# The opening of a decoder block in written order: norm weights spread by TensorE, small products ordered by readiness

## The chip, the core and the metric

The kernel runs on one core of one Trainium2 chip. The time is the device time of one execution in microseconds (us). A profile is one execution recorded by the hardware profiler: what each engine did and when. TensorE (PE) multiplies matrices and also transposes, by a product with the identity; VectorE (DVE), ScalarE (ACT) and GpSimd (POOL) do elementwise work; SyncE (SP) issues transfers (DMA). PSUM is the memory that TensorE writes.

## The reference, cut to what matters

A block with two attention branches on 528 rows (16 meta tokens ahead of 512 tokens), width 1024. The change concerns only how `u` comes about, and the columns of the common projection that are needed first: `cq` (256), `ckv` (128), `k_pe_raw` (32) and `f_logit` (16), 432 columns together, called the small projection here. `fq` and `fk` follow it.

```
u = rmsnorm(h, pre_norm_g[l])
proj = u @ w_in[l]
(cq, ckv, k_pe_raw, z_mla, fq, fk, fv, f_logit, z_fox, gate_a, gate_b) = jnp.split(proj, split_idx, axis=-1)

q = (rmsnorm(cq, mla_q_norm_g[l]) @ w_uq[l])...
kv = (rmsnorm(ckv, mla_kv_norm_g[l]) @ w_ukv[l])...
k_pe = rope(k_pe_raw, pos)[:, None]
...
log_f = jax.nn.log_sigmoid((f_logit + fox_forget_b[l]).astype(jnp.float32)).transpose(0, 2, 1)
cum = jnp.cumsum(log_f, axis=-1)
```

## The kernel before

Products of float32 are made as three: both factors are split into a high part (a cast to fp32r by ACT) and a low part (the difference, by `split_lo`, L118), and high·high, high·low and low·high are added up in one accumulator. Names ending in `h` and `l` are these parts. A product's two inputs stand behind the arrow, its accumulator ahead of it: `psm<-wsh,uTl` is a product of the small projection.

The opening goes over five tiles of rows: T0 to T3 with 128 tokens each, T4 with the 16 meta rows. Each tile passes these steps:

- `ht` is loaded; ACT sums its squares into `st`, DVE multiplies by the root and by the norm's weights `gb` and gets `hn`.
- TensorE transposes `hn` in two halves of four blocks into `pt` (PSUM, two buffers); ACT casts the high part `uTh`, DVE subtracts for the low part `uTl`.
- 24 products (8 pieces of the width, three each) give `psm` (PSUM, two buffers): 432 columns, for T4 only 176. Its weights `wsh` and `wsl` are made from `wsr`, which comes in four chunks.
- ACT sums the squares of psm's parts, DVE normalizes them and makes the rotary terms `tm`, all into `sm`.
- TensorE transposes `sm` into `pc` (PSUM, one buffer: a 48-row piece and up to three of 128). ACT and DVE take from it `cTh`, `cTl`, `kpT` and `fT`.

In front of and between these lie the products of the first pair of heads: `fq` (24 products, 512 wide) and `fk` (two halves of 24 products, 272 and 256 wide), whose weights come as `wraw` and are split into `wh` (ACT) and `wl` (POOL). Behind them come `v`, `pg`, `ppe` and the rest, whose accumulators are taken in turn from one pool of three (`accp`), fq and fk included. `fa` and `ch` are the forget gates' logarithms and their running sum (a scan on DVE), `KPH` and `KPL` the parts of `kpT`, `hlk` the parts of `fk`.

`gb` needs the same 1024 weights on all 128 partitions; two DMAs on SP's queue, behind T0's rows, write them there (0.5 MB). The low parts `wsl` go by turns to POOL and DVE. The code of the opening calls whole steps (`front`, `back`) tile by tile, in the order T0, T1, T4, T2, T3, and the scheduler sets the order in which each engine gets the instructions.

Of the kernel before, what the change touches and what calls it, by code (L numbers as in the profile page):

```python
# [54 lines left out]
def block_kernel(ctx: ExitStack, tc: tile.TileContext, x, meta_tokens, pre_norm_g, w_in, fox_forget_b,  # L55
# [38 lines left out]
    def tps(*a):  # L94
        nc.tensor.transpose(*a)
# [21 lines left out]
    def split_lo(eng, lo, src, hi):  # L117
        eng.tensor_tensor(out=lo, in0=src, in1=f32(hi), op=ALU.subtract)  # L118
# [171 lines left out]


    lctx = ExitStack()
    with ExitStack() as ph:
# [27 lines left out]
        wsh = pa1.tile([128, KD, NSM], F32R, tag="wsh", name="wsh")  # L321
        wsl = pa1.tile([128, KD, NSM], F32R, tag="wsl", name="wsl")
        nsm0 = NSM - NH
        for c in range(4):
# [6 lines left out]
            nc.scalar.copy(hi, r)
# [15 lines left out]
        def rstd(dst, ss, n, epsc, rows):
            nc.scalar.activation(dst, ss, AF.Sqrt, bias=eps_t[:rows, epsc : epsc + 1], scale=1.0 / n)
# [2 lines left out]
        def front(t):
            rows, d0 = (128, META + 128 * t) if t < 4 else (META, 0)
            ht = hts[t]
            hn = pa.tile([128, D], F32, tag="hn", name=f"hn{t}")
            st1 = pa.tile([128, 16], F32, tag="st1", name=f"st1_{t}")
            parts = [slice(0, D)]
            if t == 0:

                parts = halves
                for i, sl in enumerate(parts):  # L360
                    nc.scalar.activation(hn[:, sl], ht[:, sl], AF.Square, accum_out=st1[:, 2 + i : 3 + i])
                nc.vector.tensor_scalar(out=st1[:, 0:1], in0=st1[:, 2:3], scalar1=1.0 / D, scalar2=EPS, op0=ALU.mult,
                                        op1=ALU.add)
                nc.scalar.activation(st1[:, 1:2], st1[:, 3:4], AF.Sqrt, bias=st1[:, 0:1], scale=1.0 / D)
                nc.vector.reciprocal(st1[:, 1:2], st1[:, 1:2])
            else:
                nc.scalar.activation(hn[:rows], ht[:rows], AF.Square, accum_out=st1[:rows, 0:1])
                rstd(st1[:rows, 1:2], st1[:rows, 0:1], D, 0, rows)
            for sl in parts:
                nc.vector.scalar_tensor_tensor(out=hn[:rows, sl], in0=ht[:rows, sl], scalar=st1[:rows, 1:2],  # L370
                                               in1=gb[:rows, sl], op0=ALU.mult, op1=ALU.mult)
            for half in range(2):
                pt = ppt.tile([128, 4, 128], F32, tag="pt", name=f"pt{t}_{half}")
                for kk in range(4):
                    k = 4 * half + kk
                    tps(pt[:, kk, :rows], hn[:rows, 128 * k : 128 * k + 128], ident[:rows, :rows])
                dh = uTh[:, 4 * half : 4 * half + 4, d0 : d0 + rows]
                dl = uTl[:, 4 * half : 4 * half + 4, d0 : d0 + rows]
                nc.scalar.copy(dh, pt[:, :, :rows])
                split_lo(nc.vector, dl, pt[:, :, :rows], dh)  # L380

        def back(t):

            rows, d0, q0 = (128, META + 128 * t, 0) if t < 4 else (META, 0, R_Q)
            psm = pps.tile([128, NSM], F32, tag="psm", name=f"psm{t}")
            passes(psm[:, q0:], lambda k: uTh[:, k, d0 : d0 + 128], lambda k: uTl[:, k, d0 : d0 + 128],
                   lambda k: wsh[:, k, :], lambda k: wsl[:, k, :], KD, slice(q0, NSM))
            sm = pa.tile([128, NSM], F32, tag="sm", name=f"sm{t}")
            st2 = pa.tile([128, 16], F32, tag="st2", name=f"st2_{t}")
            for a, b, i in ((0, R_Q, 0), (R_Q, R_Q + R_KV, 1)):  # L390
                if a < q0:
                    continue
                nc.scalar.activation(sm[:rows, a:b], psm[:rows, a:b], AF.Square, accum_out=st2[:rows, i : i + 1])
                rstd(st2[:rows, 2 + i : 3 + i], st2[:rows, i : i + 1], b - a, 0, rows)
                nc.vector.scalar_tensor_tensor(out=sm[:rows, a:b], in0=psm[:rows, a:b], scalar=st2[:rows, 2 + i : 3 + i],
                                               in1=gq[:rows, a:b], op0=ALU.mult, op1=ALU.mult)
            k0 = R_Q + R_KV
            tm = pa.tile([128, 2, 2, 16], F32, tag="tm", name=f"tm{t}")
            for i in range(2):
                for cs in range(2):  # L400
                    nc.vector.tensor_tensor(out=tm[:rows, i, cs], in0=psm[:rows, k0 + 16 * i : k0 + 16 * i + 16],
                                            in1=rt[:rows, t, 2 * i + cs], op=ALU.mult)
            nc.vector.tensor_tensor(out=sm[:rows, k0 : k0 + 32].rearrange("p (a b) -> p a b", a=2), in0=tm[:rows, 0],
                                    in1=tm[:rows, 1], op=ALU.add)
            nc.scalar.copy(sm[:rows, k0 + 32 :], psm[:rows, k0 + 32 :])
            pc = pps.tile([128, 4, 128], F32, tag="pc", name=f"pc{t}", bufs=1)
            i0 = q0 // 128
            for i in range(i0, 3):
                tps(pc[:, i, :rows], sm[:rows, 128 * i : 128 * i + 128], ident[:rows, :rows])
            tps(pc[0 : ROPE + NH, 3, :rows], sm[:rows, k0:NSM], ident[:rows, :rows])  # L410
            ds = slice(d0, d0 + rows)
            nc.scalar.copy(cTh[:, i0:3, ds], pc[:, i0:3, :rows])
            split_lo(nc.vector, cTl[:, i0:3, ds], pc[:, i0:3, :rows], cTh[:, i0:3, ds])
            nc.scalar.copy(kpT[:, ds], pc[0:ROPE, 3, :rows])
            nc.scalar.activation(fT[:, ds], pc[ROPE : ROPE + NH, 3, :rows], AF.Identity, bias=fb)
# [14 lines left out]
        nc.vector.scalar_tensor_tensor(out=fa[:, 1], in0=fT, scalar=0.0, in1=fa[:, 0], op0=ALU.min, op1=ALU.subtract)  # L430
        nc.vector.tensor_tensor_scan(out=fa[:, 0], data0=fa[:, 1], data1=fa[:, 2], initial=0.0, op0=ALU.add,
# [811 lines left out]
```

## Time and profile before

| | us |
|---|---|
| median of 3 runs | 623.63 (622.18 to 624.98) |
| the profiled execution's own time | 623.18 |
| its span | 621.3 |
| PE busy in the span | 600.1 (97%) |
| ACT busy | 384.0 (62%) |
| DVE busy | 381.8 (61%) |
| POOL busy | 188.9 (30%) |

The span goes from the first to the last recorded instruction; 1.9 us of the execution lie around it. Rows of the timeline read: start, duration, engine, line, operation, out<-in, partitions x elements, count, and in brackets the idle time of the engine before it with what ended it. Rows of groups give busy time and mean nanoseconds of one, then the idle time ahead. Rows of the chain give start, length and group.

### The profile page before, as it was taken

Reading aid. Unit: us, or ns where it says so; the run is one execution under the profiler, and the core shown is the slowest. Engines: PE = TensorE matmul, PEld = TensorE weight load, DVE = VectorE, ACT = ScalarE, POOL = GpSimd, SP = SyncE. Lnnn points to the kernel's source line nnn. Section 1 sums busy time; section 2 is a strip of 40 time slices with the busy share of each in tenths; the row PEclk is TensorE's granted clock in tenths of the full one; section 3 lists DMA queues with packets and bytes.
Section 4 is the critical chain, followed back from the end, with each engine's and each line's share of the span. In section 5 each row is a group of like instructions: output and inputs, shape, how many; then the busy total and the mean of one; then the engine's idle time right before and its main releaser. Section 6 shows DMA issues by size and latency. Waiting matters only on the chain.

```text
span 621.3 us, 11569 instructions
## 1 busy us (share of the span) xinstructions
PE 600.1 (97%) x4058; PEld 492.9 (79%) x4058; DVE 381.8 (61%) x1015; ACT 384.0 (62%) x838; POOL 188.9 (30%) x237
## 2 busy tenths in 40 slices
PE   3999999999999999999999999999999999999996
PEld 2879787978988889889889888887888865565885
DVE  3746668367466566674774774676977865556133
ACT  5656677379477576774884784776767654444421
POOL 3234544634444353352444353420000000003700
PEclk9999999999999999999999999999999999999998
DMA  8442576876666577467357586567252137332202
GB/s 284 129 85 52 128 139 175 188 192 163 161 136 140 142 148 157 125 167 180 97 142 172 137 145 161 137 162 216 66 157 80 35 89 250 101 111 93 102 34 103
DMA packets 204842, 85.15 MB, mean 137 GB/s; under 512 B 122788, under 2 KB 197924, under 8 KB 204784
## 3 DMA queue, kind: packets, MB, share of 16 engines
q1 hardware_dynamic: 204784, 84.41, 53.7%
q8 instruction: 32, 0.52, 0.4%
q14 instruction: 26, 0.21, 0.1%
HBM read 54.95 MB, written 4.00 MB: 95 GB/s over the span
## 4 chain that ended last, share of the span: by engine, by line
PE 88%; ACT 3%; DMA 3%; DVE 3%; POOL 2%; issue 1%; SPq 0%; DVEq 0%; ACTq 0%; POOLq 0%
PE pg L92 14%; PE z L92 13%; PE v L92 8%; PE st L92 7%; PE po L92 7%; PE fq L92 7%; PE fk L92 7%; PE py L92 6%; PE ov L92 5%; PE yx L92 3%; PE psm L92 3%; DMA wraw<-in_w_in_dram 2%; PE yy L92 2%; PE mq L92 2%; ACT wh L142 1%; PE mk L92 1%
## 5 line engine op out<-in xcount | busy, mean ns | idle before, releaser
L118 POOL TENSOR_TENSOR wl<-wraw,wh 128x1024 fp32r<-128x1024 f32 (+1 forms) x60 | 133.0, 2219 | 299.2 <-ACT wh L142 288.3
L142 ACT CAST wh<-wraw 128x1024 fp32r<-128x1024 f32 (+1 forms) x74 | 72.9, 986 | 84.8 <-issue 35.3
L708 ACT ACTIVATE sf<-sf,nb 128x144 f32<-128x144 f32 (+3 forms) x128 | 71.9, 565 | 3.4 <-DVE nb L698 3.4
L736 ACT ACTIVATE pn<-sf,ri 128x128 f16<-128x128 f32 (+3 forms) x128 | 61.9, 551 | 15.2 <-ACT sf L708 13.8
L737 DVE SCALAR_TENSOR_TENSOR pn<-sf,ri,pn 128x128 f16<-128x128 f32 (+3 forms) x128 | 65.6, 554 | 7.4 <-ACT pn L736 7.4
L92 PE MATMUL pg<-uTh,wh 128*128 128x512 f32 x128 | 51.9, 406 | 0.0
L92 PE MATMUL z<-uTh,wh 128*128 128x512 f32 x128 | 50.9, 398 | 0.0
L92 PE MATMUL z<-uTh,wl 128*128 128x512 f32 x128 | 50.1, 392 | 0.0
L92 PE MATMUL z<-uTl,wh 128*128 128x512 f32 x128 | 50.1, 391 | 0.0
L92 PE MATMUL pg<-uTh,wl 128*128 128x512 f32 x128 | 50.0, 391 | 0.0
L92 PE MATMUL pg<-uTl,wh 128*128 128x512 f32 x128 | 49.9, 390 | 0.0
L92 PE MATMUL st<-hlk,hlq 64*128 64x272 f32 (+3 forms) x480 | 48.6, 307 | 1.1 <-DVE nb L698 0.9
L698 DVE CUSTOM_DVE_ANT_0 sf<-st,maskt 128x272 f32<-128x272 f32 (+2 forms) x128 | 48.4, 434 | 0.0
L92 PE MATMUL py<-g,yw 128*128 128x512 f16 x192 | 42.6, 379 | 0.6 <-DVE yw L1006 0.6
L92 PEld LDWEIGHTS st<-hlk,hlq 64*128 64x128 f32 x480 | 35.7, 185 | 8.1 <-DVE nb L698 2.6
L92 PE MATMUL fk<-uTl,wh 128*128 128x256 f32 (+1 forms) x128 | 36.6, 286 | 0.0
L92 PE MATMUL v<-uTh,wh 128*128 128x256 f32 (+1 forms) x128 | 36.5, 285 | 0.0
L92 PE MATMUL fk<-uTh,wh 128*128 128x256 f32 (+1 forms) x128 | 36.5, 285 | 0.0
L92 PE MATMUL fk<-uTh,wl 128*128 128x256 f32 (+1 forms) x128 | 36.5, 285 | 0.0
L92 PE MATMUL v<-uTl,wh 128*128 128x256 f32 (+1 forms) x128 | 36.4, 285 | 0.0
L92 PE MATMUL v<-uTh,wl 128*128 128x256 f32 (+1 forms) x128 | 36.4, 285 | 0.0
L92 PEld LDWEIGHTS <-yw 128*128 128x128 f16 x192 | 17.8, 97 | 22.7 <-DVE yw L1006 1.1
(291 smaller groups left out, 1503.3 us busy)
## 6 DMA issues: line engine op xcount, KB each, us to landing
wraw<-in_w_in_dram SPq DMA_DIRECT2D x56, 512.0 KB
yraw<-in_w_br_fox_dram SPq DMA_DIRECT2D x8, 512.0 KB
yraw<-in_w_br_mla_dram SPq DMA_DIRECT2D x8, 512.0 KB
wraw<-in_w_out_dram SPq DMA_DIRECT2D x8, 512.0 KB
pt<-pn SPq DMA_TRANSPOSE x128
xr<-in_x_dram SPq DMA_DIRECT2D x4, 512.0 KB
out_dram<-yo SPq DMA_DIRECT2D x8, 256.0 KB
QP<-qpe_dram SPq DMA_DIRECT2D x7, 256.0 KB
```

What stands on the lines that cost most here:

```text
L92: nc.tensor.matmul(*a, **k)
L118: eng.tensor_tensor(out=lo, in0=src, in1=f32(hi), op=ALU.subtract)
L142: nc.scalar.copy(wh[:, :n], raw[:, :n])
L698: nc.vector.tensor_tensor_reduce(out=sf_of(h, b)[:, c0 : c0 + w], in0=ps[h][:, o : o + w], in1=maskt[:, m0 : m0 + w], scale=-scale, scalar ...
L708: nc.scalar.activation(sf, sf, AF.Exp, bias=sums["nb"][:, h, b : b + 1], scale=-1.0, accum_out=sums["su"][:, h, b : b + 1])
L736: nc.scalar.activation(hi, sf, AF.Copy, scale=rib)
L737: nc.vector.scalar_tensor_tensor(out=lo, in0=sf, scalar=rib, in1=hi, op0=ALU.mult, op1=ALU.subtract)
```

## The change

The opening stands under a manual schedule: on PE, ACT, DVE, POOL and SP the instructions now run in the order in which the code is written. The steps of a tile are cut into `square`, `norm`, `turn` (transposes), `psm`, `sums`, `norms` and `back`, and the code calls them one by one. Further:

- The norm's weights are loaded as one row, `grow` (4 KB), by ACT's DMA queue. TensorE multiplies a column of ones with it: `gb[0]`, `gb[1]`, two products 512 wide in PSUM, in two of the three accumulators. Ahead of them stand four products of ones (`dark`) whose result is not used; they take the third.
- `hn` is made in halves for every tile, since `gb` is in two PSUM tiles.
- The 24 products of the small projection go by chunk of the weights: high·high, low·high, high·low; for T0 the last two chunks' products with `wsl` come at the end.
- `wsl` of chunk 0 is made by POOL, of chunks 1 to 3 by DVE; the low parts of the first fq and fk weights (`qu.make`, `ku.make`) by DVE instead of POOL.
- Of one psm, ACT makes both sums and roots first (`sums`), then DVE both normalizations (`norms`); before they took turns.
- The tiles go in the order T0, T1, T2, T3, T4, and fq begins behind T4's psm.

```diff
+        ph.enter_context(tc.manual_schedule(engines={E_.PE, E_.Activation, E_.DVE, E_.Pool, E_.SP}))
...
+        grow = pa1.tile([1, D], F32, tag="grow", name="grow")
+        nc.scalar.dma_start(grow, pre_norm_g[0:1])
...
-        gb = pa1.tile([128, D], F32, tag="gb", name="gb")
-        for sl in halves:
-            nc.sync.dma_start(gb[:, sl], pre_norm_g[0:1, sl].broadcast_to([128, 512]))
...
-        qk = q_fox(0) + k_fox(0)
-        for f, t in ((front, 0), (front, 1), (back, 0), (front, 4), (front, 2), (back, 1), (front, 3), (back, 2)):
-            f(t)
-        run(qk[:3])
-        back(3)
-        run(qk[3:7])
-        back(4)
...
+        ORD = [(k, c) for c in range(4) for k in ("hh", "lh", "hl")]
...
+        dark = acc("dark")
+        for _ in range(4):
+            mm(dark, ALL1, ALL1.unsqueeze(1).broadcast_to([128, 4, 128]), start=True, stop=True)
+        gb = [acc(f"gb{i}") for i in range(2)]
+        for i, sl in enumerate(halves):
+            mm(gb[i], one, grow[:, sl], start=True, stop=True)
+
+        T[0].square()
+        w_hi(0)
+        w_lo(0, nc.gpsimd)
+        T[0].norm()
+        low = [T[0].turn(i) for i in range(2)]
...
+        T[3].psm(ORD[8:])
+        qu.make(nc.vector)
+        T[4].psm(ORD)
+        T[2].back()
+        T[3].sums()
+        ku.make(nc.vector)
+        T[3].norms()
+        run(q0[:4])
+        T[4].sums()
+        T[4].norms()
+        T[3].back()
+        run(q0[4:])
+        T[4].back()
         nc.scalar.activation(fa[:, 0], fT, AF.Abs)
         nc.scalar.activation(fa[:, 0], fa[:, 0], AF.Exp, scale=-1.0)
+        run(k0[:8])
...
-        run(qk[7:])
+        run(k0[8:])
```

Four places show what this moves. On ACT, around the last two tiles' `back`, before the change (`pc_419` and `psm_444` are T2's pc and T3's psm, `pc_486` T3's pc):

```order
L412 CAST cTh<-pc_419 128x3x128
L414 COPY kpT<-pc_419 32x128
L415 ACTIVATE fT<-pc_419,fb 16x128
L393 ACTIVATE sm_469,st_3_470<-psm_444 128x256
L348 ACTIVATE st_3_470<-st_3_470,eps_t 128x1
L393 ACTIVATE sm_469,st_3_470<-psm_444 128x128
L348 ACTIVATE st_3_470<-st_3_470,eps_t 128x1
L405 COPY sm_469<-psm_444 128x16
L412 CAST cTh<-pc_486 128x3x128
```

And after it (`pc_493` is T2's pc, `psm_396` T3's psm, `wh_464` and `wh_509` the high parts of fq's and fk's weights):

```order
L142 CAST wh_464<-wraw_257 128x1024
L453 CAST cTh<-pc_493 128x3x128
L455 COPY kpT<-pc_493 32x128
L456 ACTIVATE fT<-pc_493,fb 16x128
L425 ACTIVATE sm_502,st_3_503<-psm_396 128x256
L426 ACTIVATE st_3_503<-st_3_503,eps_t 128x1
L425 ACTIVATE sm_502,st_3_503<-psm_396 128x128
L426 ACTIVATE st_3_503<-st_3_503,eps_t 128x1
L428 COPY sm_502<-psm_396 128x16
L142 CAST wh_509<-wraw_322 128x1024
```

The order of the steps is the same here; what is new is fk's `wh` right behind T3's sums, and that T2's pc, for which the first `cTh` waits, now stands behind T4's products on TensorE.

On DVE, the same place before:

```order
L118 TENSOR_TENSOR cTl<-pc_419,cTh 128x3x128
L349 RECIPROCAL st_3_470<-st_3_470 128x1
L395 SCALAR_TENSOR_TENSOR sm_469<-psm_444,st_3_470,gq 128x256
L349 RECIPROCAL st_3_470<-st_3_470 128x1
L395 SCALAR_TENSOR_TENSOR sm_469<-psm_444,st_3_470,gq 128x128
L401 TENSOR_TENSOR tm_479<-psm_444,rt 128x16 x4
L403 TENSOR_TENSOR sm_469<-tm_479 128x32
L118 TENSOR_TENSOR cTl<-pc_486,cTh 128x3x128
```

And after:

```order
L118 TENSOR_TENSOR wl_465<-wraw_257,wh_464 128x1024
L118 TENSOR_TENSOR cTl<-pc_493,cTh 128x3x128
L118 TENSOR_TENSOR wl_510<-wraw_322,wh_509 128x1024
L436 TENSOR_TENSOR tm_513<-psm_396,rt 128x16 x4
L438 TENSOR_TENSOR sm_502<-tm_513 128x32
L442 RECIPROCAL st_3_503<-st_3_503 128x1
L443 SCALAR_TENSOR_TENSOR sm_502<-psm_396,st_3_503,gq 128x256
L442 RECIPROCAL st_3_503<-st_3_503 128x1
L443 SCALAR_TENSOR_TENSOR sm_502<-psm_396,st_3_503,gq 128x128
```

Fk's low part `wl_510` now stands between T2's `cTl` and T3's normalization.

On TensorE, the pieces of T3's pc (`pc_486`) lay one by one between products of fq and of T4's psm (`psm_507`) before:

```order
L92 MATMUL fq_434<-uTh,wh_430 128x512
L95 MATMUL pc_486<-ident,sm_469 128x128 x2
L92 MATMUL fq_434<-uTl,wh_430 128x512
...
L92 MATMUL fq_434<-uTh,wl_431 128x512
L95 MATMUL pc_486<-ident,sm_469 128x128
L92 MATMUL psm_507<-wsh,uTh 128x176
L92 MATMUL psm_507<-wsl,uTh 128x176
L95 MATMUL pc_486<-ident,sm_469 48x128
```

After, T4's psm (`psm_468`) comes first, then T2's pc, twelve products of fq, and T3's pc (`pc_549`) in one piece:

```order
L92 MATMUL psm_468<-wsl,uTh 128x176 x2
L95 MATMUL pc_493<-ident,sm_425 48x128
L95 MATMUL pc_493<-ident,sm_425 128x128 x3
L92 MATMUL fq_523<-uTh,wh_464 128x512
...
L92 MATMUL fq_523<-uTh,wl_465 128x512
L95 MATMUL pc_549<-ident,sm_502 48x128
L95 MATMUL pc_549<-ident,sm_502 128x128 x3
L92 MATMUL fq_523<-uTh,wh_464 128x512
```

Twelve products now stand between T2's pc and T3's, and twelve behind; before, 21 of fq's 24 stood ahead of the end of T4's psm.

On DVE behind the opening, `hlk` of fk's second half (`fk_606` before, `fk_622` after) has changed places with the scan and `ch`. Before:

```order
L430 SCALAR_TENSOR_TENSOR fa<-fT,fa 16x528
L118 TENSOR_TENSOR hlk_603<-fk_606,hlk_603 128x256
L431 SCALAR_TENSOR_TENSOR fa<-fa 16x528
L435 SCALAR_TENSOR_TENSOR ch<-fa,ch 16x528
L606 TENSOR_REDUCE vsc_730<-v_705 128x1
```

After:

```order
L541 SCALAR_TENSOR_TENSOR fa<-fT,fa 16x528
L542 SCALAR_TENSOR_TENSOR fa<-fa 16x528
L546 SCALAR_TENSOR_TENSOR ch<-fa,ch 16x528
L118 TENSOR_TENSOR hlk_607<-fk_622,hlk_607 128x256
L716 TENSOR_REDUCE vsc_747<-v_722 128x1
```

The subtraction that frees fk's second accumulator now stands behind the scan (the second `fa` row) and `ch`.

More of the change, by code (lines that the diff above doesn't have):

```diff
@@ L292, in block_kernel @@
     lctx = ExitStack()
+    E_ = mybir.EngineType
     with ExitStack() as ph:
+        ph.enter_context(tc.manual_schedule(engines={E_.PE, E_.Activation, E_.DVE, E_.Pool, E_.SP}))
         pa = ph.enter_context(tc.tile_pool(name="pa", bufs=2))
@@ L345, in block_kernel, with w_hi, w_lo @@
         kpT = pal.tile([ROPE, L], F32, tag="kpT", name="kpT")
+        wsh = pa1.tile([128, KD, NSM], F32R, tag="wsh", name="wsh")
+        wsl = pa1.tile([128, KD, NSM], F32R, tag="wsl", name="wsl")
+        def w_hi(c):
+            nc.scalar.copy(wsh[:, 2 * c : 2 * c + 2, :], wsr[c])
+        def w_lo(c, eng=nc.vector):
+            sl = slice(2 * c, 2 * c + 2)
+            split_lo(eng, wsl[:, sl, :], wsr[c], wsh[:, sl, :])
         def rstd(dst, ss, n, epsc, rows):
@@ L349, in rstd @@
             nc.vector.reciprocal(dst, dst)
[L351 to L373, printed above, removed]
@@ L374, in front @@
                 for kk in range(4):
                     k = 4 * half + kk
[L376 to L415, printed above, removed]
@@ new lines, in turn, with psm @@
+                return self.low
+            def psm(self, plan):
+                q0 = self.q0
+                if not hasattr(self, "ps"):
+                    self.ps = pps.tile([128, NSM], F32, tag="psm", name=f"psm{self.t}")
+                    self.n = 0
+                us = slice(self.d0, self.d0 + 128)
+                for kind, c in plan:
+                    for k in (2 * c, 2 * c + 1):
+                        u, w = ((uTh, uTl)[kind[0] == "l"], (wsh, wsl)[kind[1] == "l"])
+                        mm(self.ps[:, q0:], u[:, k, us], w[:, k, q0:], start=(self.n == 0), stop=(self.n == 3 * KD - 1))
+                        self.n += 1
@@ new lines, in sums @@
+            def sums(self):
+                t, r, q0, psm = self.t, self.rows, self.q0, self.ps
+                self.sm = sm = pa.tile([128, NSM], F32, tag="sm", name=f"sm{t}")
+                self.st2 = st2 = pa.tile([128, 16], F32, tag="st2", name=f"st2_{t}")
+                for a, b, i in ((0, R_Q, 0), (R_Q, R_Q + R_KV, 1)):
+                    if a >= q0:
+                        nc.scalar.activation(sm[:r, a:b], psm[:r, a:b], AF.Square, accum_out=st2[:r, i : i + 1])
+                        nc.scalar.activation(st2[:r, 2 + i : 3 + i], st2[:r, i : i + 1], AF.Sqrt, bias=eps_t[:r, 0:1],
+                                             scale=1.0 / (b - a))
+                nc.scalar.copy(sm[:r, R_Q + R_KV + ROPE :], psm[:r, R_Q + R_KV + ROPE :])
@@ new lines, in back @@
+            def back(self):
+                t, r, q0, sm, ds = self.t, self.rows, self.q0, self.sm, self.ds
+                pc = pps.tile([128, 4, 128], F32, tag="pc", name=f"pc{t}", bufs=1)
+                i0, k0 = q0 // 128, R_Q + R_KV
+                tps(pc[0 : ROPE + NH, 3, :r], sm[:r, k0:NSM], ident[:r, :r])
+                for i in range(i0, 3):
+                    tps(pc[:, i, :r], sm[:r, 128 * i : 128 * i + 128], ident[:r, :r])
+                nc.scalar.copy(cTh[:, i0:3, ds], pc[:, i0:3, :r])
+                split_lo(nc.vector, cTl[:, i0:3, ds], pc[:, i0:3, :r], cTh[:, i0:3, ds])
+                nc.scalar.copy(kpT[:, ds], pc[0:ROPE, 3, :r])
+                nc.scalar.activation(fT[:, ds], pc[ROPE : ROPE + NH, 3, :r], AF.Identity, bias=fb)
@@ new lines, in block_kernel @@
+        w_hi(0)
+        w_lo(0, nc.gpsimd)
+        T[0].norm()
+        low = [T[0].turn(i) for i in range(2)]
+        low[0]()
+        low[1]()
+        w_hi(1)
+        w_lo(1)
+        T[1].square()
+        w_hi(2)
+        w_hi(3)
+        T[0].psm(ORD[:6])
+        T[1].norm()
+        T[0].psm([("hh", 2), ("lh", 2)])
+        low = [T[1].turn(i) for i in range(2)]
+        w_lo(2)
+        w_lo(3)
+        T[0].psm([("hh", 3), ("lh", 3), ("hl", 2), ("hl", 3)])
+        low[0]()
+        low[1]()
@@ new lines, in block_kernel @@
+        T[2].square()
+        qu.load()
+        T[1].psm(ORD[:4])
+        T[0].sums()
+        T[2].norm()
+        T[1].psm(ORD[4:8])
+        low = [T[2].turn(i) for i in range(2)]
+        low[0]()
+        T[0].norms()
+        low[1]()
+        T[1].psm(ORD[8:])
+        T[3].square()
+        ku.load()
+        T[2].psm(ORD[:3])
+        T[3].norm()
+        T[0].back()
+        T[2].psm(ORD[3:8])
+        T[1].sums()
+        low = [T[3].turn(i) for i in range(2)]
+        low[0]()
+        T[1].norms()
@@ new lines, in block_kernel @@
+        low[1]()
+        T[2].psm(ORD[8:])
+        T[4].square()
+        T[3].psm(ORD[:5])
+        T[1].back()
+        T[4].norm()
+        T[3].psm(ORD[5:8])
+        T[2].sums()
+        low = [T[4].turn(i) for i in range(2)]
+        low[0]()
+        low[1]()
+        T[2].norms()
+        T[3].psm(ORD[8:])
[7 more added lines that the diff above has]
+        T[4].sums()
```

79 lines of the change are left out of this document (66 added, 13 removed).

## The prediction

> **What bounds the kernel now.** I read the stretches of the span first, then the chain of waits of the first 72 us, then the groups and the timeline of the opening. The columns of the stretches are from:to, length, and busy us (with instructions) of PE, PEld, DVE, ACT and POOL, then PEclk, DMA share and GB/s.
>
> ```profile
> 0.00:22.60 22.60, 11.80 (x43) 10.08 (x44) 10.90 (x14) 11.47 (x21) 7.43 (x16) 1.00 0.79 260
> 22.60:51.10 28.50, 26.77 (x156) 22.56 (x156) 16.08 (x51) 17.44 (x55) 7.12 (x3) 1.00 0.30 66
> 51.10:58.40 7.30, 7.29 (x55) 6.77 (x55) 5.27 (x12) 6.15 (x14) 5.11 (x10) 1.00 0.25 40
> 58.40:69.60 11.20, 11.20 (x74) 10.24 (x73) 7.76 (x15) 4.70 (x9) 4.01 (x3) 1.00 0.34 99
> 69.60:615.40 545.80, 543.03 (x3737) 443.28 (x3735) 339.90 (x921) 343.48 (x738) 165.25 (x205) 1.00 0.56 138
> ```
>
> 22.60 is where tile 0's small products (psm) are read, 51.10 where tile 4's psm ends, 58.40 where v begins, 69.60 where pg ends. From 58.40 to 615.40 TensorE idles 2.8 us in 557. So what moves v's first product moves the end by as much, and the change is worth what it does to that one moment, plus what it puts into the pg stretch. TensorE idles 10.8 us before 22.60 and 1.7 us from there to 58.40: the gain to be had is in the first stretch.
>
> ```profile
> 3.38 0.63 ACT L361 ACTIVATE hn<-ht 128x512 f32<-128x512 f32 x1 [1.17 <-DMA ht<-in_x_dram]
> 6.88 0.75 DVE L370 SCALAR_TENSOR_TENSOR hn<-ht,st,gb 128x512 f32<-128x512 f32 x1 [1.65 <-DMA gb<-in_pre_norm_g_dram]
> 10.60 0.91 ACT L331 CAST wsh<-wsr 128x864 fp32r<-128x864 f32 x1 [0.30 <-DMA wsr<-in_w_in_dram]
> 11.55 1.77 DVE L118 TENSOR_TENSOR wsl<-wsr,wsh 128x864 fp32r<-128x864 f32 x1 [2.90 <-ACT wsh L331]
> 7.78 2.04 PE L95 MATMUL pt<-ident,hn 128*128 128x128 f32 x8 [7.78 <-DVE hn L370]
> L118 DVE TENSOR_TENSOR uTl<-pt,uTh 128x512 fp32r<-128x512 f32 x8 | 5.3, 685 | 1.7 <-ACT uTh L379 1.7
> 13.98 4.33 PE psm L92 x11
> 41.82 2.95 PE psm L92 x15
> 48.65 2.43 PE psm L92 x22
> 37.67 1.84 PE fq L92 x8
> 53.97 4.44 PE fk L92 x35
> ```
>
> The start waits for x's first half (3.38), for gb by DMA (1.65 us on DVE), then for wsr by DMA; TensorE is dense from 13.98. The last four rows (start, us, group) give TensorE's prices at full rate: a 432-wide psm product 0.197, a 176-wide one 0.11, fq 0.23, fk 0.127.
>
> **The change, part by part.** My sums come from one walk through the written order: an instruction starts at the latest of its engine's last end and its inputs' ends, and lasts what its row says. The same walk through the old order puts v at 58.62 (58.41 in the chain of waits) and pg's end at 70.05 (69.60), so it is 0.2 to 0.5 late, and I compare walk with walk.
>
> *gb from one row.* Two DMAs and their 1.65 us wait go; 0.5 MB less stands ahead of wsr in SP's queue. DVE's first hn can then start at 5.3 instead of 6.88. In exchange six products enter TensorE, ahead of T0's transposes, and a 4 KB transfer enters ACT's queue; its issue lies in the 1.17 us that ACT waits for x. I take the row as landed with x's first half, at 3.4. The 512-wide float32 product of one row has no row here: between a psm product at half rate (0.36 below, so 0.43 for 512 columns) and four times that, both are done between 4.3 and 6.8, the first half's between 3.8 and 5.1, and hn0 begins at 5.3 or little later. I take 5.5, since the cheap end is nearer to the psm row. The meta tile's transfer goes behind x's third tile on SP; its norm now comes last, so nobody waits for it.
>
> *Small weights.* DVE now makes three low parts instead of two, before T0's last products: hn0 in halves of 0.75, two uTl of 0.69, wsl 1.77 three times, hn1 in halves of 0.75, in all 9.5 us (ends overlap the next start a little), with about 1.4 us of waiting for the transposes and uTh between hn0 and uTl. From 5.5 that is 16.4, and two products of 0.2 need the last wsl: 16.8 summed up, 16.3 in the walk with the overlaps. I take 16.3 for the end of T0's psm (15.3 when wsl keeps 1.77 and gb is early, 16.8 when it lasts longer beside POOL). Before, it was read at 22.6: 6.3 us gained.
>
> *The middle, psm0 to psm4.* TensorE has 72 products of 0.197 and 24 of 0.11 (16.8 us), three tiles' transposes and two backs (together about 4.2): 21.0 us. In the walk it waits four times: 1.05 for psm's second buffer behind T0.norms, 1.7 behind T1.norms, 1.4 for T4's hn behind T1's cTl, 0.9 behind T2.norms; 5.05 in all. So psm4 ends at 42.4. The bounds of these waits are 1.7, which is what the old order idles from 22.6 to 58.4, and 6. Before, 21 of the 24 fq products lay inside this part as filler; none does now.
>
> *From psm4 to v.* What is left is pc2 0.5, 24 fq 5.57, pc3 0.5, pc4 0.25, 48 fk 5.95, in sum 12.8; before it was 7.3, busy throughout. To this comes a wait. T3's sums stand behind T2.back on ACT, T2.back needs psm4 done on TensorE, and between T3's sums and T3's norms the written order puts ku.make. The links are these:
>
> ```profile
> 37.70 0.48 ACT L412 CAST cTh<-pc 128x384 fp32r<-128x384 f32 x1 [0.83 <-PE pc L95]
> 38.22 0.56 DVE L118 TENSOR_TENSOR cTl<-pc,cTh 128x384 fp32r<-128x384 f32 x1 [0.96 <-ACT cTh L412]
> 38.81 0.25 ACT L414 COPY kpT<-pc 32x128 f32<-32x128 f32 x1 [0.43 <-DVE cTl L118]
> 39.08 0.36 ACT L415 ACTIVATE fT<-pc,fb 16x128 f32<-16x128 f32 x1
> 44.79 0.38 ACT L393 ACTIVATE sm<-psm 128x256 f32<-128x256 f32 x1 [1.20 <-PE psm L92]
> 45.30 0.29 ACT L348 ACTIVATE st<-st,eps_t 128x1 f32<-128x1 f32 x1
> L142 ACT CAST wh<-wraw 128x1024 fp32r<-128x1024 f32 x4 | 4.2, 1058 | 0.0
> L118 DVE TENSOR_TENSOR wl<-wraw,wh 128x1024 fp32r<-128x1024 f32 x14 | 17.1, 1223 | 10.1 <-ACT wh L142 10.0
> 47.34 0.35 DVE L395 SCALAR_TENSOR_TENSOR sm<-psm,st,gq 128x128 f32<-128x128 f32 x1
> 47.61 0.41 DVE L401 TENSOR_TENSOR tm<-psm,rt 128x16 f32<-128x16 f32 x4
> 45.89 0.48 DVE L395 SCALAR_TENSOR_TENSOR sm<-psm,st,gq 128x256 f32<-128x256 f32 x1
> ```
>
> After pc2: cTh 0.48, cTl 0.56, kpT 0.25, fT 0.28 net, the four sums and the copy 1.4 (two squares of 0.38 and 0.28, two roots of 0.29), wh 1.06, wl 1.2, tm 0.41 and its sum 0.2, then 0.48 and 0.35 with two reciprocals: about 7.0 us in sum, 6.3 in the walk, where ends overlap the next start, until pc3 can run. Twelve fq products cover 2.8. TensorE waits 3.55 there, 0.47 for pc3's last input and 0.23 at T4.back: 4.25. So v begins at 42.4 + 12.8 + 4.25 = 59.4; by the walk's unrounded numbers 59.3 (58.3 to 59.8 by psm0's bounds), against 58.62: **+0.7**. The 6.3 us won at the start go into 3.3 us more waiting in the middle and 4.25 at T3.back. wl1 and wl2, which POOL made before, cost DVE 1.2 each; only wl2 lies on the path. POOL's queue gets shorter, and nothing waits for it here.
>
> *In front of pg.* The low part of fk's second half now stands behind the scan and ch; pg takes that accumulator.
>
> ```profile
> L503 DVE CAST KPH<-kpT 32x528 fp32r<-32x528 f32 x3 | 3.7, 1222 | 0.6 <-ACT fT L415 0.6
> 61.04 1.68 DVE L430 SCALAR_TENSOR_TENSOR fa<-fT,fa 16x528 f32<-16x528 f32 x1
> 62.65 0.41 DVE L118 TENSOR_TENSOR hlk<-fk,hlk 128x256 fp32r<-128x256 f32 x1
> 62.98 1.24 DVE L431 TENSOR_TENSOR_SCAN fa<-fa 16x528 f32<-16x528 f32 x1
> 64.25 0.64 ACT L434 ACTIVATE ch<-fa 16x528 fp32r<-16x528 f32 x1 [3.61 <-DVE fa L431]
> 64.93 0.70 DVE L435 SCALAR_TENSOR_TENSOR ch<-fa,ch 16x528 fp32r<-16x528 f32 x1 [0.71 <-ACT ch L434]
> ```
>
> From T4.back on DVE has four KPH of 1.0 to 1.2, two KPL, hlk, fa 1.68, scan 1.24, ch 1.4 with ACT's part, hlk 0.41: done 0 to 1.0 us after v's 48 products. I take 0.5, since KPH alone can move it by 0.8.
>
> *The clock.* PEclk reads 1.00 all through the opening, yet the spacing of equal products does not stay the same:
>
> ```profile
> 16.66 0.56 PE L92 MATMUL psm<-wsh,uTh 128*128 128x432 f32 x1
> 17.02 0.56 PE L92 MATMUL psm<-wsl,uTh 128*128 128x432 f32 x1
> 20.27 0.36 PE L92 MATMUL psm<-wsh,uTh 128*128 128x432 f32 x1
> 20.47 0.36 PE L92 MATMUL psm<-wsl,uTh 128*128 128x432 f32 x1
> 615.00:615.50 0.50, 0.33 (x3) 0.12 (x2) 0.00 (x0) 0.09 (x1) 0.00 (x0) 1.00 0.00 0
> 617.00:617.50 0.50, 0.00 (x0) 0.00 (x0) 0.50 (x2) 0.00 (x0) 0.00 (x0) 0.79 0.00 0
> 617.50:618.00 0.50, 0.00 (x0) 0.00 (x0) 0.36 (x1) 0.00 (x0) 0.00 (x0) 0.50 0.00 0
> ```
>
> One product every 0.36 us until 19.9, every 0.20 from there: TensorE starts at half rate, and at the end the granted clock falls to 0.50 at 617.3 (a mean of 0.79 over the half us), about 1.95 us after the last product (615.33). The wait at T3.back is 3.55, longer than that. So I expect TensorE to come out of it at half rate. How long that lasts has no row; the start gives bounds. Twice the idle that sufficed, or 3.4 us of slow products, costs 1.7; dense from 13.98 to the change at 19.9 was 5.9 us, and with the small breaks at pc3 and pc4 up to 6.8, costs 3.4. Products at half rate cover 0.5 of the small waits that I had counted. I take 2.1, the middle less that.
>
> [...]
>
> **The sum**, against the profiled execution's own 623.18 (0.45 under the 623.63 of the runs): 623.18 + 0.7 + 0.5 + 2.1 = 626.5. Half a per cent is 3.1 us, about what a measurement of this kernel can tell from no change, so the bounds are 620.5 and 626.7.
>
> **The rivals.**
>
> *The wait is there, the clock holds.* 624.4. For it: the fall at the end is one observation, and at the start 5.9 us passed from dense work to the change, so the clock needn't answer a short break at once. Against it: 3.55 is nearly twice 1.95.
>
> *Faster.* The wait at T3.back is not there, because T3's sums and norms come out by the time the twelve fq products are done. Its place is ACT between T2.back and ku.make; its price is 4.25 us, and 623.18 + 1.2 − 4.25 = 620.1. It decides when the chain from pc2 to pc3 is under 2.8 us instead of 6.3; wh and wl would have to leave it (2.3) and T2.back's copies to overlap (1.6). The order speaks against it: in it wl2 stands ahead of T3's norms on DVE. The same sign comes from the middle: at 1.7 instead of 5.05 us of waits v would be at 56, and the time 621.0 with the wait and 623.1 with the clock falling too.
>
> *The start stays at half rate.* The four products of ones take 1.7 us at half rate and the two for gb 0.9 or more; then TensorE waits for hn0 until about 7. If that doesn't raise the clock, psm0 and part of psm1 run at 0.36: twenty products more at +0.16 make 3.3 us, so 627.7 without the fall at T3.back and 629.8 with it. For it: from 7.8 to 9.8 TensorE worked and the products from 13.98 were slow all the same. Against it: psm0 is paced by DVE, so slow products hide up to 16.3 and are dense enough there to raise the clock.
>
> **Chances.** Wait and falling clock 0.48 (its own range 625.0 to 628.5); wait, clock holds 0.27; faster 0.15; slow start 0.10. The range of 8 in 10 goes from 620.8 to 629.0. Half of the likeliest case and all of the slow start lie above 626.7: slower 0.38; the other half, the clock that holds and the middle's small gains: same 0.49; faster 0.13.
>
> **What the profile would show.** Right: psm of tile 0 ends near 16; TensorE waits for DVE's sm ahead of pc3 for over 3 us, and the chain before it reads cTh, cTl, kpT, sm, wh, wl, tm, sm; fq products after it are 0.43 apart, not 0.23; v begins between 59 and 62; pg waits under 1 us on hlk. Wrong: psm0 at 19 or later, no idle time at pc3, products 0.23 apart behind it, or v before 57. What would overturn the forecast most easily is the clock: one spacing, 2.1 us.

## The result, and the profile after

The changed kernel takes 630.03 us (median of 5 runs, 628.0 to 630.47), the kernel before 623.93 in the same comparison: a ratio of 1.0089, interval 1.0062 to 1.0116. It is slower by about 6 us; the prediction said 626.5, with 620.8 to 629.0 as its range. The profiled execution is the fastest of the five: 628.0, span 626.2, 4.9 over the span before.

The stretches after are cut at the ends of T0's psm, of T4's psm, at v's first product and at pg's end; columns as before.

```profile
0.00:16.22 16.22, 15.00 (x49) 10.02 (x49) 8.81 (x14) 10.91 (x19) 4.54 (x16) 1.00 0.92 302
16.22:41.89 25.67, 21.09 (x129) 18.85 (x128) 14.32 (x46) 12.68 (x43) 0.00 (x0) 1.00 0.16 44
41.89:61.66 19.77, 14.44 (x84) 12.08 (x84) 10.53 (x25) 11.30 (x29) 7.47 (x10) 0.91 0.37 72
61.66:74.60 12.94, 11.75 (x75) 10.58 (x74) 7.70 (x14) 5.02 (x9) 4.43 (x5) 1.00 0.48 138
74.60:620.30 545.70, 542.72 (x3736) 442.72 (x3735) 340.27 (x921) 343.40 (x738) 165.20 (x205) 1.00 0.55 137
```

T0's psm ends at 16.22 and T4's at 41.89, 9.0 us earlier than before (50.92). All of it and more is lost between there and v: v's first product starts at 61.66 instead of 58.25 (+3.4) and the first one behind pg at 74.44 instead of 69.56 (+4.9), all by the starts of their rows; the rest of the span lasts 551.7 as against 551.8. What TensorE waited for from its first product to 75 us (total, times, longest):

```profile
PE pc L95 <- DVE st L442: 5.2, 1, 5.2
PE psm L92 <- DVE sm L443: 3.4, 3, 1.8
PE pg L92 <- DVE hlk L118: 1.2, 1, 1.2
PE pt L95 <- DVE hn L393: 1.2, 2, 0.9
```

The waits of the middle add up to 4.6 (1.07, 1.76, 0.9 + 0.27, 0.57). The longest is T3's pc. Its row names `st`, DVE's reciprocal right behind the rotary sum; the columns that pc's first piece reads are that sum's. On DVE and POOL the last links are these:

```profile
46.69 1.23 DVE L118 TENSOR_TENSOR wl<-wraw,wh 128x1024 fp32r<-128x1024 f32 x1 [3.09 <-ACT wh L142]
47.84 0.41 DVE L436 TENSOR_TENSOR tm<-psm,rt 128x16 f32<-128x16 f32 x4
48.28 2.03 DVE L438 TENSOR_TENSOR sm<-tm 128x32 f32<-128x32 f32 x1
47.93 2.34 POOL L118 TENSOR_TENSOR wl<-wraw,wh 128x1024 fp32r<-128x1024 f32 x1 [38.54 <-DVE wl L118]
```

A sum of 32 columns takes 2.03 us, and ends at 50.3 with POOL's subtraction for v's weights, which began 0.35 ahead of it. The same pair stood in the trace before, where the sum took 1.38 and ended 0.06 behind POOL:

```profile
35.88 1.38 DVE L403 TENSOR_TENSOR sm<-tm 128x32 f32<-128x32 f32 x1
34.82 2.38 POOL L118 TENSOR_TENSOR wl<-wraw,wh 128x1024 fp32r<-128x1024 f32 x1 [0.43 <-ACT wh L142]
```

Behind the wait TensorE runs at half rate for a while; the last row is the wait in front of pg:

```profile
50.46 1.43 PE L95 MATMUL pc<-ident,sm 128*48 128x128 f32 x4 [5.21 <-DVE st L442]
52.54 0.63 PE L92 MATMUL fq<-uTh,wl 128*128 128x512 f32 x1
52.97 0.63 PE L92 MATMUL fq<-uTh,wh 128*128 128x512 f32 x1
54.28 0.40 PE L92 MATMUL fq<-uTl,wh 128*128 128x512 f32 x1
54.51 0.40 PE L92 MATMUL fq<-uTh,wl 128*128 128x512 f32 x1
68.86 0.50 PE L92 MATMUL pg<-uTh,wh 128*128 128x512 f32 x1 [1.19 <-DVE hlk L118]
```

Fq products stand 0.43 apart up to 53.8, then 0.23. From the start of T3's pc to that of T4's it takes 5.07 us here and 3.96 in e3_fill (below), where T3's pc starts at the same moment and the clock holds: the clock costs 1.1 in this execution. At full rate and without any wait it takes 3.49 (e6_order, below); the 0.47 between 3.49 and 3.96 is pc's pieces waiting one by one for DVE's normalization.

### The profile page after: what moved, and what is told of

Its sections match the earlier page's. It is cut to its first block, busy times and chain, and to the rows that moved or that the text cites. A ratio compares the mean times of both kernels' runs of the same rounds, so it can differ in the third digit from the quotient of the medians.

```text
span 626.2 us, 11590 instructions
## 1 busy us (share of the span) xinstructions
PE 605.1 (97%) x4066; PEld 494.3 (79%) x4066; DVE 383.5 (61%) x1022; ACT 384.1 (61%) x838; POOL 181.6 (29%) x235
## 4 chain that ended last, share of the span: by engine, by line
PE 83%; DVE 3%; ACT 1%; DMA 1%; issue 1%; SPq 1%; DVEq 0%; ACTq 0%
PE pg L92 14%; PE z L92 13%; PE st L92 7%; PE v L92 7%; PE po L92 7%; PE fk L92 7%; PE fq L92 6%; PE py L92 6%; PE ov L92 5%; PE yx L92 3%; PE yy L92 2%; PE mq L92 2%; DMA qpe_dram<-gT 1%; PE mk L92 1%; PE vt L95 1%; PE ppe L92 1%
## 5 line engine op out<-in xcount | busy, mean ns | idle before, releaser
L118 POOL TENSOR_TENSOR wl<-wraw,wh 128x1024 fp32r<-128x1024 f32 (+1 forms) x58 | 127.9, 2208 | 316.7 <-ACT wh L142 270.9
```

## The experiments

In each, times are medians, and the ratio is to the kernel before, run beside it.

**The change once more** (e0_again, no edit).

> The changed kernel itself, unchanged. Its profiled execution was the fastest of five (628.0; the others 629.4 to 630.5, at mean granted clocks of 0.991 to 0.993 instead of 0.995). Theory P (what varies is how long TensorE stays at half rate behind the wait for T3's pc, and nothing else): all engines do the same to within 0.1 us up to that wait; the 432- and 512-wide products stand at half rate (fq 0.43 apart) for 2 to 7 us, and each us of such products makes the span longer by half a us; median 629.5 to 630.5. Rival Q: the fq spacing is as in the first profile (0.43 for five products), and a longer span comes from elsewhere (a DMA, a wait in the middle).

629.76 us, ratio 1.0086 (1.0070 to 1.0102). The profiled execution was the slowest of six (631.0), and shows one way in which executions part. TensorE's rows of it:

```profile
10.11 0.73 PE L92 MATMUL psm<-wsl,uTh 128*128 128x432 f32 x2
37.59 0.74 PE L92 MATMUL psm<-wsl,uTh 128*128 128x432 f32 x2
47.74 0.53 PE L92 MATMUL fq<-uTl,wh 128*128 128x512 f32 x1
52.92 1.43 PE L95 MATMUL pc<-ident,sm 128*48 128x128 f32 x4 [3.72 <-DVE st L442]
58.00 0.52 PE L92 MATMUL fq<-uTh,wh 128*128 128x512 f32 x1
```

The clock rose in the row at 10.11, fell in that at 37.59, rose again in that at 47.74, fell in the wait at T3's pc and rose at 58.0. So it fell here already behind the waits of the middle, ahead of T4's psm, and once more at T3's pc. The wait at T3's pc is shorter (3.72), since slower products cover more of it; v begins at 65.07, 3.4 later than in the first profile. Up to 37 us TensorE's rows stand within 0.5 us of that profile. Theory P holds in part: the half rate behind T3's pc lasted for some nine products of fq instead of five. But the engines did not agree to 0.1 us up to there, and it is not only the wait at T3's pc that lets the clock fall.

**V's weights split later** (e1_v_weights_late). POOL's subtraction leaves the place beside T3's norms.

```diff
+        wv = win_w(O_FV, 0)
...
         ku.load()
+        wv.load()
...
         T[3].back()
+        wv0 = wv()
...
-                get, nk, act = win_w(O_FV, pr), KD, u_act
+                get, nk, act = win_w(O_FV, pr) if pr else (lambda: wv0), KD, u_act
```

> The changed kernel, but v's weights (cast by ACT, low part by POOL) are split behind T3.back instead of at T3's norms. In the profile of the changed kernel DVE's 32-wide sum of T3's rotary terms took 2.03 us instead of 0.19 and ended with POOL's subtraction. Theory A (that sum waits for POOL, as both of its inputs are in SBUF): it takes 0.19 here, pc of T3 starts 1.8 us earlier, TensorE's wait ahead of it is 3.4 instead of 5.2; the clock still falls there; v begins 1.5 to 2.2 earlier, time 1.5 to 2.2 under the changed kernel's. Rival B (the sum is slow for its own place in the queue, after the 128x1024 subtraction): still 2.0, wait 5.2, time as the changed kernel's.

628.09 us, ratio 1.0066 (1.0047 to 1.0085): 1.7 to 1.9 under the changed kernel's two medians. DVE's sum and TensorE's pc:

```profile
47.85 0.19 DVE L438 TENSOR_TENSOR sm<-tm 128x32 f32<-128x32 f32 x1
48.19 0.27 PE L95 MATMUL pc<-ident,sm 128*48 128x128 f32 x1 [3.37 <-DVE st L442]
```

0.19 instead of 2.03, and 3.37 instead of 5.21: theory A. The clock fell in this shorter wait too (a mean of 0.89 from 48 to 49 us), and fq behind it stands 0.43 apart up to 51.98. The run also shows the walk of the prediction at work: without POOL, the wait is the 3.55 worked out there, within 0.2. `tm`, with one input in PSUM, kept its 0.41 beside POOL in the changed kernel (47.84, POOL from 47.93); the sum, with both inputs in SBUF, did not keep its 0.19. What in the chip holds it up is not shown.

**T3's norms ahead of T2.back** (e2_norms_first).

```diff
-        T[2].back()
         T[3].sums()
-        ku.make(nc.vector)
         T[3].norms()
+        T[2].back()
+        ku.make(nc.vector)
```

> The changed kernel, but T3's sums and norms stand ahead of T2.back, and fk's weights (ku.make) behind it. Theory A (the wait for T3's pc of 5.2 us, with what it does to the clock, is the whole loss in this stretch, and stands on the written order alone): no wait over 0.3 at T3's pc, fq 0.23 apart throughout, up to 1.3 us of a new wait at T4's pc (its rotary sum meets POOL's subtraction); v begins at 55 to 56 instead of 61.7; pg still waits about 1.2 for the low part of fk's second half; time 621 to 623, 7 to 9 under the changed kernel's median. Rival C (another input of pc comes late next, such as fq's or fk's weights): a wait of 2 to 4 us moves to fq or fk, time 624 to 627.

625.06 us, ratio 0.9995 (0.9976 to 1.0014): 4.7 to 5 under the changed kernel, level with the kernel before; 621 to 623 was expected, so the gain as a median is smaller. The profiled execution (622.41):

```profile
44.72 0.60 PE L95 MATMUL pc<-ident,sm 128*48 128x128 f32 x4
46.22 2.39 POOL L118 TENSOR_TENSOR wl<-wraw,wh 128x1024 fp32r<-128x1024 f32 x1 [36.19 <-ACT wh L142]
46.87 1.78 DVE L438 TENSOR_TENSOR sm<-tm 16x32 f32<-16x32 f32 x1
50.27 0.26 PE L95 MATMUL pc<-ident,sm 16*48 16x16 f32 x2 [2.22 <-ACT fT L456]
```

T3's pc has no wait left. POOL's subtraction now meets T4's rotary sum (1.78 as against 0.18 in e1_v_weights_late), which keeps DVE from T3's `cTl` until 49.03; ACT's `kpT` and `fT` follow, and only then is the one buffer of pc free for T4's, which waits 2.22. v begins at 56.41, 5.25 earlier. Of the 12 executions five lie at 622.4 to 623.0, the others at 625.0 to 627.7, at mean clocks of 0.988 to 0.996: the clock still falls in many.

**Products to fill the wait** (e3_fill). 24 products of data, not used, ahead of T3's pc.

```diff
+        fill = acc("fill")
+        for _ in range(24):
+            mm(fill[:, :NSM], uTh[:, 0, META : META + 128], wsh[:, 0, :], start=True, stop=True)
         T[3].back()
```

> The changed kernel, with 24 products more, 432 wide, of data that are there (their result isn't used), between fq's twelfth product and T3's pc. They take 4.7 us, less than the wait of 5.2 that stands there, so T3's pc comes no later. Theory A (the wait lets the clock fall, which costs 1.8 us in the profiled execution and more in the others): pc and fq behind it run at full rate (0.23 apart), v begins 1.8 earlier than in the profile of the changed kernel, and the median is 2 to 4 under the changed kernel's, 626 to 627.5. Rival D (the half rate behind the wait comes from something else, such as ACT's or POOL's work beside it): fq 0.43 apart still, time 629 to 630.5.

627.09 us, ratio 1.0044 (1.0028 to 1.0061): 2.7 to 2.9 under the changed kernel by adding work.

```profile
50.43 0.27 PE L95 MATMUL pc<-ident,sm 128*48 128x128 f32 x1 [0.47 <-DVE st L442]
52.25 0.39 PE L92 MATMUL fq<-uTh,wh 128*128 128x512 f32 x1
52.48 0.39 PE L92 MATMUL fq<-uTl,wh 128*128 128x512 f32 x1
```

pc starts at the same moment (50.43 and 50.46), and fq runs 0.23 apart at once. So the half rate behind the wait comes from TensorE's idleness there (5.21 us without the 24 products, 0.47 with them). It costs 2.7 to 2.9 as a median, but 1.1 in the first profile: v begins at 60.52 here instead of 61.66, and 1.8 earlier was expected.

**The same with products of ones** (e3b_ones).

```diff
+        fill = acc("fill")
+        for _ in range(22):
+            mm(fill, ALL1, ALL1.unsqueeze(1).broadcast_to([128, 4, 128]), start=True, stop=True)
         T[3].back()
```

> The changed kernel with 22 products of ones (bf16, 512 wide, 4.7 us, result not used) between fq's twelfth product and T3's pc, in place of the 24 products of data of e3_fill. If products of ones count as work for the clock, fq behind T3's pc runs 0.23 apart and the median is as e3_fill, 626.5 to 627.5. If they don't (at the start four of them, then gb's two products and eight transposes, 7.4 us without a break, left TensorE at half rate), fq runs 0.43 apart and the median is 629 to 630.5.

628.08 us, ratio 1.0053 (1.0034 to 1.0072). In the profile the clock fell in the middle, as in the change run once more, and had risen before the wait; behind the products of ones it was still up:

```profile
53.67 0.60 PE L95 MATMUL pc<-ident,sm 128*48 128x128 f32 x4
54.57 0.39 PE L92 MATMUL fq<-uTh,wl 128*128 128x512 f32 x1
54.80 0.39 PE L92 MATMUL fq<-uTh,wh 128*128 128x512 f32 x1
```

Products of ones kept the clock here: fq behind them stands 0.23 apart. The median is 1.0 above the one with data; three of six executions have clocks of 0.990 to 0.996. The profile at 0.990 has its fall in the middle; the others were not traced, and the two medians don't settle more.

**Without the products of ones at the start** (e8_no_dark).

```diff
-        dark = acc("dark")
-        for _ in range(4):
-            mm(dark, ALL1, ALL1.unsqueeze(1).broadcast_to([128, 4, 128]), start=True, stop=True)
```

> The changed kernel without its four idle products of ones at the start. In both profiles of the changed kernel the clock rose only at 10.2 and 12.6, behind psm products. Theory: the products of ones do nothing for it; gb's products start when the row has landed, at about 3.0 as before, T0's transposes at 6.7 to 6.8, T0's psm ends at 15.7 to 16.3; time as the changed kernel's, within 0.5. Rival: without them the clock rises 3.4 us later, T0's psm ends up to 1.5 later, time 1 to 1.5 more.

629.78 us, ratio 1.0080 (1.0060 to 1.0101): as the changed kernel. TensorE's start:

```profile
3.03 3.75 PE L92 MATMUL gb<-grow,one 1*128 1x512 f32 x4 [3.03 <-DMA grow<-in_pre_norm_g_dram]
11.82 0.69 PE L92 MATMUL psm<-wsh,uTl 128*128 128x432 f32 x2
```

gb's products start when the row has landed, as with the four ahead of them, and the clock rises in the row at 11.82. The products of ones bring nothing here.

This profile is also the nearest there is to the changed kernel's median execution (629.96 us, mean clock 0.993; seven of that kernel's eleven executions show 0.993). Its rows behind T3's wait:

```profile
50.23 1.43 PE L95 MATMUL pc<-ident,sm 128*48 128x128 f32 x4 [5.19 <-DVE st L442]
56.15 0.56 PE L92 MATMUL fq<-uTh,wl 128*128 128x512 f32 x1
62.78 0.29 PE L92 MATMUL v<-uTh,wh 128*128 128x272 f32 x1
```

The clock held in the middle. Behind T3's pc all twelve fq products stand 0.43 apart, where in the first profile five did. From pc to v it takes 12.55 us, against 11.20 there and 10.09 in e3_fill: the clock costs 2.5 instead of 1.1.

**hlk ahead of the scan** (e5_hlk_early), in the changed kernel.

```diff
+        run(k0[8:])
         nc.vector.tensor_tensor_scan(out=fa[:, 0], data0=fa[:, 1], data1=fa[:, 2], ...
...
-        run(k0[8:])
```

> The changed kernel, with the second half of fk (and its hlk) written ahead of the scan, as the order stood before. Theory (pg's wait of 1.2 us is for that hlk, behind scan and ch): pg follows v without a wait, time 1.0 to 1.4 under the changed kernel's (628.3 to 629 as a median). Rival (pg would wait for v's weights or another buffer all the same): a wait of over 0.5 stays, time as the changed kernel's.

628.24 us, ratio 1.0065 (1.0049 to 1.0081), 1.5 to 1.8 under the changed kernel. The profile is of the slowest of four executions (629.53), with the long half rate of the last profile behind T3's wait:

```profile
68.54 0.28 PE L92 MATMUL v<-uTh,wl 128*128 128x256 f32 x1
68.66 0.40 PE L92 MATMUL pg<-uTh,wh 128*128 128x512 f32 x1
```

pg follows v at once.

**The better order** (e6_order). T3's and T4's sums and norms ahead of fk's weights, and hlk ahead of the scan.

```diff
-        T[2].back()
         T[3].sums()
-        ku.make(nc.vector)
         T[3].norms()
-        run(q0[:4])
         T[4].sums()
+        T[2].back()
         T[4].norms()
+        ku.make(nc.vector)
+        run(q0[:4])
...
+        run(k0[8:])
         nc.vector.tensor_tensor_scan(out=fa[:, 0], data0=fa[:, 1], data1=fa[:, 2], ...
```

> The changed kernel with T3's sums and norms, and T4's, ahead of fk's weights: sums of T3, norms of T3, sums of T4, T2.back, norms of T4, then ku.make; and the second half of fk (with its hlk) written ahead of the scan. Theory A: the waits at T3's pc and at T4's pc (2.2 us with only T3 moved, where T4's rotary sum met POOL's subtraction and took 1.78) are both gone, v begins at 54.0 to 54.6, pg waits nothing; 620.3 to 621.5 in executions in which the clock holds, and 2.5 to 3.5 more in those in which it falls in the middle (T2's and T3's psm), as with only T3 moved; median 621 to 624. Rival: pc waits for something else (T2.back's copies), gain under 1 us against the run with only T3 moved.

619.69 us, ratio 0.9932 (0.9910 to 0.9954): faster than both kernels, 10 us under the changed one, and a little better than expected as a median.

```profile
44.86 0.60 PE L95 MATMUL pc<-ident,sm 128*48 128x128 f32 x4
48.35 0.26 PE L95 MATMUL pc<-ident,sm 16*48 16x16 f32 x2
54.49 0.29 PE L92 MATMUL v<-uTh,wh 128*128 128x272 f32 x1
```

No wait at either pc, v at 54.49, 7.2 ahead of the changed kernel. Four of six executions lie at 619.0 to 619.9, two at 622.1 and 622.6, at clocks of 0.996.

**The same, kept busy in the middle** (e9_warm). 19 products, not used, in the four waits of the middle.

```diff
+        warm_pe(5)
         T[2].psm(ORD[:3])
...
+        warm_pe(8)
         T[3].psm(ORD[:5])
...
+        warm_pe(4)
         low = [T[4].turn(i) for i in range(2)]
...
+        warm_pe(2)
         T[4].psm(ORD)
```

> The kernel of e6_order, with 19 more products of 432 columns, their result not used, where TensorE waits between T1's psm and T4's psm: 5, 8, 4 and 2 in waits of 1.07, 1.76, 0.9 + 0.27 and 0.57 us. Theory W (the spread of 2.5 to 3.5 us between executions is the clock falling in a stretch of 3.41 us of which these waits take half): all executions lie within 1.5 us of each other, mean granted clock 0.998 or more, median 620 to 621.5, best one as the best of e6_order. Rival: the spread stays (it comes from the start, where the clock rises at different moments), median as e6_order.

619.74 us, ratio 0.9920 (0.9901 to 0.9939), clocks of 0.998 or 0.999 in all five. Four lie at 618.9 to 620.3, and one at 622.15; this one was profiled, and has its 2.1 us at one place far behind the opening, where TensorE waits for nothing that the profile shows:

```profile
PE ov L92 <- issue: 2.1, 1, 2.1
```

By these clocks it no longer falls in the middle. But the executions still lie 3.2 apart where 1.5 was expected, and the intervals of the two versions overlap: that this one is the faster isn't shown.

**gb by DMA** (e7_gb_by_dma), on the better order.

```diff
         load_h(0)
+        gbt = pa1.tile([128, D], F32, tag="gb", name="gb")
+        for sl in halves:
+            nc.sync.dma_start(gbt[:, sl], pre_norm_g[0:1, sl].broadcast_to([128, 512]))
+        gb = [gbt[:, sl] for sl in halves]
         load_w(0)
...
-        for i, sl in enumerate(halves):
-            mm(gb[i], one, grow[:, sl], start=True, stop=True)
```

> The kernel of e6_order with gb spread by two DMAs on SP behind T0's rows, as before the change, and without gb's two products (the products of ones stay). Theory (what the start gains comes from the 0.5 MB that no longer stand ahead of the small weights): ACT's first wsh is cast at 9.4 instead of 6.3, the last chunk's low part ends 2 to 3 later, T0's psm ends at 17.3 to 18.5 instead of 16; all of it stays to the end, time 1.5 to 3 over e6_order. Rival (the gain of the start is the written order's, not gb's): T0's psm ends within 0.7 of e6_order's, time within 1 us of it.

624.48 us, ratio 0.9995 (0.9978 to 1.0011), 4.8 over the same order with gb from TensorE. ACT's first cast, with gb by DMA and, in the second row, from TensorE:

```profile
9.64 0.91 ACT L355 CAST wsh<-wsr 128x864 fp32r<-128x864 f32 x1 [4.07 <-DMA wsr<-in_w_in_dram]
```

```profile
6.64 0.91 ACT L355 CAST wsh<-wsr 128x864 fp32r<-128x864 f32 x1 [1.43 <-DMA wsr<-in_w_in_dram]
```

The 0.5 MB cost 3.0 us here and 3.4 at the end of T0's psm (19.35 against 15.97); v begins 4.2 later, 0.8 of it from a fall of the clock in the middle. The theory holds, with more than it expected (18.5 at the latest, 3 us at the most). T0's psm still ends 3.2 ahead of the kernel before (22.6), so the row through TensorE is worth about half of what the start gains. As a median it is worth all by which e6_order leads the kernel before.

## Why the prediction was wrong, step by step

- *The start* was right: T0's psm ended at 16.22 (16.3 forecast), by luck in part. Two terms of it were off and cancelled: gb's two products took 3.78 instead of between 0.9 and 3.4, and `wsl` on DVE about 1.0 instead of the 1.77 that it took beside POOL.
- *The middle* was right: 4.6 us of waits (5.05), T4's psm done at 41.89 (42.4).
- *From psm4 to v* is the step that failed. The mechanism was right: the wait stands at T3's pc, behind the chain that was named. A term of the chain was mis-sized: "tm 0.41 and its sum 0.2" took 0.41 and 2.03, and the wait was 5.21 for the 3.55 worked out. The prediction held that "POOL's queue gets shorter, and nothing waits for it here". But with DVE making wl1 and wl2, what POOL splits at that moment is v's weights, and the sum waits for it; without that the median is 1.7 to 1.9 lower (e1_v_weights_late). The price stood in the trace of before, in the row of 1.38 at 35.88. The other terms of this stretch fit: 12.83 us from T4's psm to v without a wait in e6_order (41.66 to 54.49; 12.8 forecast), and 0.47 for pc3's later inputs (0.47 forecast). The 0.23 at T4.back did not come.
- *In front of pg* is mis-sized too: 0.5 forecast, 1.19 of waiting measured, and the first product behind pg is 1.5 further behind than v. Undone alone it gave 1.5 to 1.8 (e5_hlk_early). The four KPH lasted 4.1 us (58.43 to 62.50), as forecast.
- *The clock* fell, as forecast. The 3.4 to 6.8 us of slow products behind the 2.1 were an estimate; the profiles showed a half rate of 3.4 us at that wait in the first one and 6.8 in e8_no_dark. The 2.1 lies between what it cost in the profiled execution (1.1) and in one like the median (2.5, e8_no_dark). V at 61.66 is close to the forecast 61.5 (59.4 and 2.1) by luck: the wait was 1.7 longer, the clock 1.0 cheaper. The sum had no term for a fall in the middle, which e0_again shows.
- *The base*: the sum starts from 623.18, the profiled execution, and the kernel before had a median of 623.93 in the comparison. These are 0.75 of the miss. The changed kernel's profiled execution in turn lies 2.0 under its median; 1.1 of that is the longer half rate, as far as e8_no_dark's profile stands for the median, and the rest was not traced.

So the sum of the forecast came to 626.5 for an execution that took 628.0 and a median of 630.0. With the sum beside POOL (+1.8), pg (+1.15) and the base (+0.75) put right it would be 630.2; that is an estimate, which adds up the results of single runs.

The rival "faster" had the right place, and its condition was not met in this order. It is met when T3's norms leave the chain behind T2.back, and 5 us go with the wait (e2_norms_first). "The clock holds" did not happen; where it was made to hold (e3_fill), the median was 627.09. The 629.8 of "the start stays at half rate" lies next to the measured 630.0 by coincidence: products stood at full rate from 13 us on, and T0's psm was on time.

Two slips of the working changed little: half of 0.48 and 0.10 make 0.34 for "slower", not 0.38, and twice 1.95 us of idle is 3.9, not 3.4.

## What to carry to other kernels

An order written by hand fixes also what stands between two links of a chain; walk the last chain ahead of each wait, and move what isn't part of it (here a weight split) behind. Beside a DVE operation with both inputs in SBUF, such as the rotary sum here, look for what POOL does at that moment, in the order after the change (that sum took 1.38 to 2.03 us beside POOL's weight split, and 0.18 to 0.19 without it). A wait of TensorE costs more than its length once the clock falls: price it with a shorter and a longer stretch of half rate behind it (1.1 and 2.5 us here), and look also at places where several short waits stand close together (in e0_again the clock fell behind them at 37.8). Start the sum from a median where executions differ, since the one that was profiled can be a fast one.
